# SSD output projection by seven products of quarters, and the SSD skip term written by ScalarE

## The chip, the cores and the metric

One NeuronCore of one Trainium2 chip runs the whole layer. The metric is the device time of one execution in microseconds (us), as the median of several runs. Five engines work at once, each through a list of instructions of its own, in order: TensorE (PE, matrix products into PSUM banks), VectorE (DVE), ScalarE (ACT), GpSimd (POOL) and SyncE (SP, which issues most DMAs). They wait for each other by semaphores. DMA engines move data between HBM and the on-chip memory.

## The reference

One decoder layer over 1024 tokens of width 1024, all in float32. An SSD (Mamba-2) branch and a latent attention branch are projected back to the model's width, weighed by gates, added, and projected once more (W_O); a gated feed-forward network (FFN) follows.

```python
y = ssd_chunked_scan(xs * dt[..., None], dt * a, bm, cm)
y = y + xs * d_skip[:, None]                      # the skip term
y = y.reshape(b, l, D_INNER) * jax.nn.silu(z)
y = rms_norm(y.reshape(b, l, SSD_GROUPS, D_INNER // SSD_GROUPS), ...)
...
y_ssd = ssd_mixer(...) @ w_ssd_proj[i]            # 1024 x 2048 by 2048 x 1024
y_mla = mla_mixer(...) @ w_mla_proj[i]
x = x + (g_ssd * y_ssd + g_mla * y_mla) @ w_o[i]
h = rms_norm(x, norm_ffn_g[i])
u = causal_depthwise_conv(h @ w_up[i], conv_ffn_w[i], conv_ffn_b[i])
x = x + (jax.nn.silu(u_gate) * u_val) @ w_down[i]
```

## The kernel before

Activations lie channel by channel: 128 channels on the partitions, 512 tokens (a "half") in the free dimension. A float32 product is made of three matmuls: each operand is split into a high part, rounded to the PE's fast format (a copy by ScalarE, L153), and a low part, the rest (a subtraction by VectorE or GpSimd, L154), and `mm3` (L174 to L177) adds high x high, high x low and low x high into one PSUM bank. So one k-step of a 128x512 tile is 3 matmuls, and both the weights and the activations must have been split before.

The order of the work is that in which the Python code records it, engine by engine. During the SSD scan a list `background` of generators (other projections) is advanced between the steps of the scan, so that PE has work while the scan's vector steps run; what a step of the scan takes from it is fixed by counts.

*The scan* runs over 4 groups of 512 channels (a tile `xg`, also called `chan`, of 128 x 4 x 1024) and in each over 8 chunks of 128 tokens. `ssd_inputs` prepares a chunk: eight exponents by ScalarE (L850, `seg`), a product of them with the scores on VectorE (L864), the chunk's inputs transposed and scaled (L855, L860). `ssd_output` (L885) adds into a PSUM bank `yp` on PE: 8 matmuls within the chunk (L891), and 8 for the carried state (L896). Then VectorE adds the skip term: four operations of 128x128, one for each block of channels, x = x * hds + yp (L903), and one of 128x512 that multiplies by the gate z (L905). `ssd_finish` normalizes a group's half. It writes it to HBM in `y_d`, and for half 0 of the last group it splits it in place. `first_ssd_tile` (L1052), the last piece of the background, makes the first projection tile of 48 matmuls while the last group is finished.

*The projection* (L1204 to L1231) runs over two halves, and in each over 8 tiles of output channels (`ct`). A tile takes 16 k-steps of 3 matmuls. Its weights come in two halves by `load_w`: 256 KB loads by SP into one of two buffers `wraw`, then the split. GpSimd's queue loads two tiles of gates, `gt` and `mt`; VectorE and ScalarE make the merged value from PSUM, `gt` and `mt` (L1224 to L1229) and split it (`m`, `ma`). After the tiles of a half comes *W_O* of that half (L1242 to L1277): 2 blocks of 512 columns, each 4 weight pairs (`kp`) by 4 token tiles by 2 k-steps, 192 matmuls; VectorE adds the product to the residual `big` (L1270). So the order is projection half 0, W_O half 0, projection half 1, W_O half 1. The normalization of half 0's new residual, `norm(x0)` (L1232 to L1234, scaled at L255), is recorded between the second projection and W_O of half 1, and eight transposes of its result (`quarter`) are spread over W_O of half 1 from the start. The activations of half 1 are loaded back from `y_d` by `load_act`, 16 tiles of 256 KB. The FFN behind is done by seven products of quarters already; its first weights (`w_raw`, `w_sums`) are loaded and added during these stages.

## Time and profile before

| | us |
|---|---|
| runs | 2203.98, 2197.95, 2196.79 |
| median | 2197.95 |
| profiled execution | 2203.12 |
| its span, first to last instruction | 2201.3 |

The three runs are timed executions; the page of the profile comes from one more execution, whose own time stands in the third row. All stretches and starts below count from the start of its span. In them the SSD scan lies from about 740 to 1262, the projection and W_O of both halves from 1253 to 1524, and the FFN behind. A line number Lnnn is one of the kernel before.

### The profile page before, as it was taken

What the parts mean: (1) busy time and instruction counts of PE and PEld (TensorE: products, weight loads), DVE (VectorE), ACT (ScalarE), POOL (GpSimd) and SP (SyncE); (2) the same over time, 40 slices, a digit from 0 to 9 for tenths busy, and PEclk for the clock granted to TensorE, in tenths of its full rate; (3) what the DMA queues carried; (4) which work ended last, traced back from release to release, by engine and by line L of the source; (5) the groups of instructions that cost most, each with busy time, mean ns of one, the idle gap of its engine ahead of it and who ended that gap; (6) DMA issues with size and microseconds to landing.
All of it is one profiled execution on the core that took longest, in us unless ns stands there. A gap on an engine that the chain in (4) does not pass through costs nothing. (4 is left out here: it accounts for less than half of the span.)

```text
span 2201.3 us, 30448 instructions
## 1 busy us (share of the span) xinstructions
PE 2145.3 (97%) x10844; PEld 1713.8 (78%) x10844; DVE 1446.8 (66%) x2567; ACT 1064.3 (48%) x2034; POOL 969.6 (44%) x1049
## 2 busy tenths in 40 slices
PE   8999999999999999999999999999899999999999
PEld 7877776777777887778877787887678888877787
DVE  4466756575664469898877746545876676676762
ACT  5445454555454456656564424324655455554330
POOL 2344424432443237665456311013377777744430
PEclk9999999999999999999999999999999999999999
DMA  4221111111112224645266566542132333248642
GB/s 147 69 69 46 40 53 64 50 35 55 64 48 88 93 82 148 195 151 172 92 229 212 178 224 200 166 161 95 63 119 92 111 105 110 96 138 330 258 158 82
DMA packets 121767, 268.97 MB, mean 122 GB/s; under 512 B 13520, under 2 KB 25744, under 8 KB 121616
## 3 DMA queue, kind: packets, MB, share of 16 engines
q1 hardware_dynamic: 105600, 214.47, 29.0%
q0 software_dynamic: 14528, 49.29, 6.8%
q10 hardware_dynamic: 1488, 3.28, 0.4%
q8 instruction: 85, 1.39, 0.3%
q14 instruction: 66, 0.54, 0.1%
HBM read 201.45 MB, written 65.54 MB: 121 GB/s over the span
## 5 line engine op out<-in xcount | busy, mean ns | idle before, releaser
L175 PE MATMUL lin<-h,whi 128*128 128x512 f32 x1440 | 591.6, 411 | 1.5 <-DVE lt L330 1.5
L177 PE MATMUL lin<-h,wlo 128*128 128x512 f32 x1440 | 563.7, 391 | 0.0
L176 PE MATMUL lin<-h,whi 128*128 128x512 f32 x1440 | 562.4, 391 | 0.0
L175 PEld LDWEIGHTS lin<-h,whi 128*128 128x128 f32 x1440 | 270.6, 188 | 83.9 <-issue 33.8
L177 PEld LDWEIGHTS lin<-h,wlo 128*128 128x128 f32 x1440 | 270.4, 188 | 59.8 <-POOL wlo L154 0.4
L176 PEld LDWEIGHTS lin<-h,whi 128*128 128x128 f32 x1440 | 271.5, 189 | 53.2 <-issue 6.7
L154 POOL TENSOR_TENSOR wlo<-wraw,whi 128x512 fp32r<-128x512 f32 x134 | 193.0, 1458 | 169.3 <-ACT whi L153 165.7
L153 ACT CAST whi<-wraw 128x512 fp32r<-128x512 f32 x232 | 141.1, 619 | 260.0 <-PE lin L176 111.1
L664 POOL TENSOR_TENSOR acc<-acc,e 128x512 f32<-128x512 f32 (+3 forms) x80 | 78.8, 984 | 246.1 <-ACT e L659 223.7
L659 ACT ACTIVATE e<-s 128x512 f32<-128x512 f32 (+1 forms) x192 | 93.3, 492 | 153.7 <-DVE s L657 133.1
L1140 DVE TENSOR_TENSOR xlo<-ur,xhi 128x512 fp32r<-128x512 f32 (+1 forms) x41 | 83.0, 2024 | 60.9 <-ACT xhi L1139 60.9
L154 DVE TENSOR_TENSOR wlo<-wraw,whi 128x512 fp32r<-128x512 f32 x98 | 70.0, 725 | 75.1 <-ACT whi L153 74.7
L850 ACT ACTIVATE seg<-abc,acum 128x128 f32<-128x128 f32 x256 | 80.2, 390 | 47.1 <-PE yp L891 41.0
L175 PE MATMUL dps<-tq,h 128*128 128x512 f32 x242 | 96.8, 400 | 5.8 <-DVE xr L1601 3.5
L176 PE MATMUL dps<-tq,h 128*128 128x512 f32 x242 | 96.9, 400 | 0.8 <-DVE tq L154 0.8
L177 PE MATMUL dps<-tq,h 128*128 128x512 f32 x242 | 96.4, 398 | 0.0
L812 DVE SCALAR_TENSOR_TENSOR xg<-craw,cl,xg 128x1024 f32<-128x1024 f32 x48 | 73.7, 1536 | 27.4 <-ACT xg L810 26.9
L664 DVE TENSOR_TENSOR acc<-acc,e 128x512 f32<-128x512 f32 (+3 forms) x80 | 55.1, 689 | 37.1 <-ACT e L659 36.5
L1216 POOL DMA_DIRECT2D mt<-m_d x16 | 8.6, 539 | 147.1 <-DVE gt L1225 97.1
L154 DVE TENSOR_TENSOR h<-ar,h 128x1024 fp32r<-128x1024 f32 (+1 forms) x35 | 56.4, 1616 | 25.4 <-ACT h L153 25.3
L670 PE MATMUL pv<-e,vt 128*64 128x512 f32 (+3 forms) x384 | 72.9, 498 | 0.0
L629 DVE CUSTOM_DVE_ANT_0 s<-s,negw 128x128 f32<-128x128 f32 (+3 forms) x128 | 62.3, 495 | 13.5 <-PE s L627 13.4
(617 smaller groups left out, 5225.7 us busy)
## 6 DMA issues: line engine op xcount, KB each, us to landing
wraw<-in_w_main SPq DMA_DIRECT2D x112, 256.0 KB
ur<-in_w_up SPq DMA_DIRECT2D x44, 512.0 KB
ar<-f_d SPq DMA_DIRECT2D x34, 512.0 KB
abc<-ac_d POOLq DMA_DIRECT2D x32, 512.0 KB, 5.3
wraw<-in_w_ssd SPq DMA_DIRECT2D x64, 256.0 KB
f_d<-wraw POOLq DMA_DIRECT2D x33, 256.0 KB, 2.4
g_d<-lt SPq DMA_DIRECT2D x32, 256.0 KB
z_d<-lt SPq DMA_DIRECT2D x32, 256.0 KB
```

The costliest lines, as they stand in the source:

```text
L153: S.copy(hi, raw)
L154: (eng or V).tensor_sub(lo, raw, hi.bitcast(F32))
L175: PE.matmul(ps, lhsT=ah, rhs=bh, start=first, stop=False, **more)
L176: PE.matmul(ps, lhsT=ah, rhs=bl, start=False, stop=False, **more)
L177: PE.matmul(ps, lhsT=al, rhs=bh, start=False, stop=last, **more)
L629: V.tensor_tensor_reduce(ps[:, 0:w], ps[:, 0:w], negw[:, 512 - w:512], 1.0, 2 * NEG, ALU.add, ALU.max, nm[:, j, i:i + 1])
L659: S.activation(e[:, c0:512], ps[:, 0:w], AF.Exp)
L664: (V if hd else G).tensor_tensor(accs[hd][:, c0:512], accs[hd][:, c0:512], e[:, c0:512], op=ALU.add)
L670: PE.matmul(pv[hd * 64:(hd + 1) * 64, c0:512], lhsT=vt[:, j, hd * 64:(hd + 1) * 64], rhs=es[hd][:, c0:512], start=first, stop=last)
L812: V.scalar_tensor_tensor(c, raw[:, k:k + T], col(cw + k), c, op0=ALU.mult, op1=ALU.add)
L850: S.activation(seg[:, hd, :], abc[:, hd, :], AF.Relu, bias=acum[:, c, 8 * g + hd:8 * g + hd + 1], scale=-1.0)
L1140: eng.tensor_sub(lo, r, hi.bitcast(F32))
```

## The change

*The projection.* Instead of two halves of 8 output tiles by 16 k-steps, the product is cut into quarters: the activations into channels of two kinds and tokens of two halves, the weights into two kinds of input channels and two halves of output tiles. Seven products of quarters (Winograd's form of Strassen's method) replace eight. For each, sums of quarters stand in for the activations ("forms": s22, and t1 to t4) and for the weights (differences and sums). They run in the order 1, 2, 7, 6, 5, 3, 4, each as 4 units of 8 k-steps, 24 matmuls of the same shape. The code loads raw quarters of weights three units ahead (`fetch`), prepares a unit's weights and gates one unit ahead (`prepare`), and combines the results after each (`finish_unit`).

```diff
+
+    def quarter_k(kk, h):
+        return 8 * (kk // 4) + 4 * (kk // 2 % 2) + 2 * h + kk % 2
+
+    def quarter_w(ct, h, kp):
+        return w_ssd[ct, kp].rearrange("p (g h j) c -> h p g (j c)", h=2, j=2)[h]
+
+    def load_q(ct, h):
+        hi = wpool.tile([P, KD, P], F32R, name="whi")
+        lo = wpool.tile([P, KD, P], F32R, name="wlo")
+        for kp in range(2):
+            raw = wpool.tile([P, 512], F32, name="wraw", bufs=2)
+            nc.sync.dma_start(out=raw.rearrange("p (g c) -> p g c", c=256), in_=quarter_w(ct, h, kp))
+            f = "p a b -> p (a b)"
+            split(raw, hi[:, 4 * kp:4 * kp + 4, :].rearrange(f), lo[:, 4 * kp:4 * kp + 4, :].rearrange(f), w_eng[0])
+        return hi, lo
+
+    def quarter_step(ps, w, t, kk, first):
+        mm3(ps, (w[0][:, kk, :], w[1][:, kk, :]), (t[:, 0, :], t[:, 1, :]), first and kk == 0, kk == KD - 1,
+            skip_group_check=True)
...
+            def ring():
+                turns[0] += 1
+                if turns[0] % 3 == 0:
+                    return up.tile([P, KD, P], F32, name="us", bufs=1)
+                return up.tile([P, T + 2], F32, name="ug", bufs=2)[:, 0:T].rearrange("p (k c) -> p k c", c=P)
...
+            e1, e2 = [ep.tile([P, 4, D], F32, name="x2").rearrange("p i (k c) -> p i k c", c=P) for _ in range(2)]
+            ur = [up.tile([P, KD, P], F32, name=f"ur{n}", bufs=2) for n in (1, 1, 2, 2)]
...
+            units = [(p, i) for p in (1, 2, 7, 6, 5, 3, 4) for i in range(4)]
...
+            source = {6: "t2", 5: "t1", 3: "22", 7: "t3", 4: "t4"}
+            following = {2: 7, 7: 6, 6: 5, 5: 3, 3: 4}
...
+                if p == 7:
+                    raw_q(ur[i], i, 0)
+                    rs[p, i] = ring()
+                    raw_q(rs[p, i], i + 4, 0)
+                elif p == 6:
+                    raw_q(e1[:, i], i + 4, 1)
...
+                if p in (1, 2, 4):
+                    ws[p, i] = load_q(i + 4 if p == 4 else i, 0 if p == 1 else 1)
+                    return
+                v = {6: e1[:, i], 5: ur[i], 3: rs.get((p, i)), 7: e2[:, i]}[p]
+                if p == 7:
+                    V.tensor_tensor(v, ur[i], rs[p, i], op=ALU.subtract)
+                elif p == 6:
+                    V.tensor_tensor(v, v, e2[:, i], op=ALU.subtract)
+                elif p == 5:
+                    V.tensor_tensor(v, v, e1[:, i], op=ALU.add)
+                else:
+                    V.tensor_tensor(v, v, e1[:, i], op=ALU.subtract)
+                hl = [wpool.tile([P, KD, P], F32R, name=w) for w in ("whi", "wlo")]
+                split(v.rearrange(flat), hl[0].rearrange(flat), hl[1].rearrange(flat))
...
+            for n in range(2, len(units)):
+                p, i = units[n]
+                prepare(n + 1)
+                fetch(n + 3)
+                f = following.get(p)
+                if f:
+                    t = forms.setdefault(f, [])
+                    for _ in range(min(3, KD - len(t))):
+                        t.append(load_act(t_d[source[f]], len(t) * P, slice(0, 512)))
...
+                for kk in range(KD):
+                    quarter_step(b, ws[p, i], forms[p][kk], kk, p in (1, 2, 7))
+                finish_unit(p, i)
```

`X` and `Z` are PSUM banks, four each; `finish_unit` copies X to on-chip memory after products 1, 6 and 5, adds partial products on VectorE after 2, 5 and 4, and makes a merged value with the gates after 7, 5, 3 and 4 (two steps on VectorE each). `first_ssd_tile` becomes `first_products`: the first two units, also 48 matmuls. The forms are made at the end of each group in `ssd_finish` (half 1 no longer goes to `y_d`, but for GpSimd's queue to five buffers in HBM):

```diff
-                else:
-                    nc.sync.dma_start(out=y_d[r0:r0 + P, s], in_=x[:, j, s])
+                elif half == 0:
+                    nc.sync.dma_start(out=y_d[r0:r0 + P, :], in_=x[:, j, s])
             if half:
+                s11, s21 = x[:, 0:2, 0:512], x[:, 2:4, 0:512]
+                s12, s22 = x[:, 0:2, 512:1024], x[:, 2:4, 512:1024]
+
+                def form(name, v, a=None, b=None, op=None):
+                    if op is not None:
+                        V.tensor_tensor(v, a, b, op=op)
+                    nc.gpsimd.dma_start(out=t_d[name][2 * g * P:2 * (g + 1) * P, :].rearrange("(j p) t -> p j t", p=P),
+                                        in_=v)
+
+                form("22", s22)
+                form("t3", s12, s22, s12, ALU.subtract)
+                form("t2", s11, s12, s11, ALU.add)
+                form("t4", s21, s21, s11, ALU.subtract)
+                form("t1", s22, s22, s11, ALU.subtract)
```

*The order behind it.* Both halves' W_O now follow each other after the last product. `norm(x0)` is recorded between them, as one group of four tiles (before, a tile at a time); the transposes of its result start six places later in W_O of half 1; the weight pairs of that half are taken in the order 2, 3, 0, 1; the weights of the FFN's second pair are added at its third weight pair.

```diff
+                    drain([norm(x0, x0, ep, x2ss[0], group=4)])
...
+                    for n_, kp in enumerate((2, 3, 0, 1) if half else range(4)):
...
+                            slot += i % 2
+                            if half and i % 2 and slot > 5 and nq < KD:
                                 quarter("11" if nq < 4 else "21", nq % 4, h2_raw(nq, 0), act_tile(), G)
```

*The skip term.* ScalarE writes x * hds into the PSUM bank while the chunk is prepared, and PE adds onto it; VectorE reads the bank in the multiplication by z.

```diff
+            yp = psy.tile([P, 512], F32, name="yp", bufs=2)
+            for j in range(4):
+                S.activation(yp[:, j * P:(j + 1) * P], xs[:, j, cs], AF.Copy, scale=hds[:, 4 * g + j:4 * g + j + 1])
+            return abc, seg, xdt, xde, bt, yp
...
-                              rhs=seg[:, hd, :], start=True, stop=c == 0)
+                              rhs=seg[:, hd, :], start=False, stop=c == 0, skip_group_check=True)
...
-            for j in range(4):
-                V.scalar_tensor_tensor(x[:, j, cs], x[:, j, cs], hds[:, 4 * g + j:4 * g + j + 1],
-                                       yp[:, j * P:(j + 1) * P], op0=ALU.mult, op1=ALU.add)
-            V.scalar_tensor_tensor(x[:, :, cs], zts.pop(0), 0.5, x[:, :, cs], op0=ALU.mult, op1=ALU.mult)
+            V.scalar_tensor_tensor(x[:, :, cs], zts.pop(0), 0.5, yp.rearrange("p (j t) -> p j t", t=P),
+                                   op0=ALU.mult, op1=ALU.mult)
...
+        seeded = [psy.tile([P, 512], F32, name="yp", bufs=2) for _ in range(2)]
+        for i in (0, 1, 0):
+            PE.matmul(seeded[i], lhsT=h[0][0][:, 0, 0:P], rhs=h[0][0][:, 0, :], start=True, stop=True)
```

Where the instructions stand: three places. In the kernel after, lines lie lower in the file: L153 and L154 are L154 and L155, L850 is L871, L852 is L873, L866 is L887. The first place is ScalarE around one chunk of the scan's second group (`seg` and `abc` belong to the chunk, `craw` and `lt` to the projections beside it). Before:

```order
L852 ACTIVATE seg<-seg 128x1024
L153 CAST whi<-wraw 128x512
L850 ACTIVATE seg<-abc,acum 128x128 x5
L816 ACTIVATE craw<-xg 128x1024
L850 ACTIVATE seg<-abc,acum 128x128
L329 ACTIVATE lt<-lin 128x512
L914 ACTIVATE sq__9247<-xg 128x512
L850 ACTIVATE seg<-abc,acum 128x128 x2
L852 ACTIVATE seg<-seg 128x1024
L866 ACTIVATE abc<-abc 128x1024
L153 CAST whi<-wraw 128x512
```

After, in the same group (L891 are the seeds):

```order
L871 ACTIVATE seg<-abc,acum 128x128 x3
L891 ACTIVATE yp<-xg,hds 128x128
L871 ACTIVATE seg<-abc,acum 128x128 x4
L891 ACTIVATE yp<-xg,hds 128x128
L873 ACTIVATE seg<-seg 128x1024
L887 ACTIVATE abc<-abc 128x1024
L891 ACTIVATE yp<-xg,hds 128x128
L350 ACTIVATE lt<-lin 128x512
L891 ACTIVATE yp<-xg,hds 128x128
L154 CAST whi<-wraw 128x512
L891 ACTIVATE yp<-xg,hds 128x128
L154 CAST whi<-wraw 128x512
```

The four `yp` rows of a chunk are new. They stand one by one between the chunk's exponents and the other work.

The second place is VectorE in the projection. Before, in a tile of half 0 (`gt`, `mt` are the gates, `lin` the PSUM bank, `m` the merged value, `wlo` the low part of the next weights):

```order
L1229 SCALAR_TENSOR_TENSOR m<-gt,m 128x512
L154 TENSOR_TENSOR wlo<-wraw,whi 128x512 x2
L1224 SCALAR_TENSOR_TENSOR gt<-gt,lin 128x512
L154 TENSOR_TENSOR wlo<-wraw,whi 128x512
L1225 TENSOR_TENSOR gt<-gt,mt 128x512
L154 TENSOR_TENSOR wlo<-wraw,whi 128x512
L1229 SCALAR_TENSOR_TENSOR m<-gt,m 128x512
```

After, in the units of product 7 (`x_12837` holds the differences of product 7, `x_12836` those of product 6, `h<-lt` is the low part of a form):

```order
L1318 SCALAR_TENSOR_TENSOR gt<-gt,mu 128x512
L1307 TENSOR_TENSOR x_12836<-x_12836,x_12837 128x1024
L155 TENSOR_TENSOR h<-lt,h 128x512 x2
L1251 SCALAR_TENSOR_TENSOR ma<-mu,ma 128x512
L155 TENSOR_TENSOR wlo<-x_12837,whi 128x1024
L1319 TENSOR_TENSOR mu<-gt,mt 128x512
L1307 TENSOR_TENSOR x_12836<-x_12836,x_12837 128x1024
L1251 SCALAR_TENSOR_TENSOR ma<-mu,ma 128x512
L1307 TENSOR_TENSOR x_12836<-x_12836,x_12837 128x1024
L1309 TENSOR_TENSOR ur_12838<-ur_12838,x_12836 128x1024
L155 TENSOR_TENSOR wlo<-x_12836,whi 128x1024
```

Sums of weights of 128x1024 now stand in the same queue as the splits that PE waits for.

The third place is VectorE at `norm(x0)`. Before, with the second projection's steps behind the scaling (L255):

```order
L247 SCALAR_TENSOR_TENSOR nst<-nst 128x1
L248 TENSOR_TENSOR nst<-nst 128x1
L249 SCALAR_TENSOR_TENSOR nst<-nst 128x1
L255 TENSOR_SCALAR x_13360<-x_13360,nst 128x1024 x2
L234 TENSOR_REDUCE nst<-sq_13362 128x1 x2
L154 TENSOR_TENSOR wlo<-wraw,whi 128x512
L1224 SCALAR_TENSOR_TENSOR gt<-gt,lin 128x512
L154 TENSOR_TENSOR wlo<-wraw,whi 128x512
L1225 TENSOR_TENSOR gt<-gt,mt 128x512
```

After, between the two W_O (L276 is the scaling, `wlo` the low part of W_O's weights, L1223 a copy of a transposed tile, L1424 the residual's sum):

```order
L268 SCALAR_TENSOR_TENSOR nst<-nst 128x4
L269 TENSOR_TENSOR nst<-nst 128x4
L270 SCALAR_TENSOR_TENSOR nst<-nst 128x4
L276 TENSOR_SCALAR x_14048<-x_14048,nst 128x1024 x4
L155 TENSOR_TENSOR wlo<-wraw,whi 128x512 x4
L1223 TENSOR_SCALAR x_14048<-dps,cl 128x4x128
L155 TENSOR_TENSOR wlo<-wraw,whi 128x512
L1424 TENSOR_TENSOR x_14049<-dps,x_14049 128x512
```

Behind the scaling of all four tiles now stand the low parts of W_O's own weights.

More of the change, by code (lines that the diff above doesn't have):

```diff
@@ L88, in tile_hybrid_layer @@
     l_d = dram.tile([4 * MH, 256], F32, name="l_d")
-    y_d = dram.tile([2 * D, T], F32, name="y_d")
+    y_d = dram.tile([2 * D, 512], F32, name="y_d")
+    t_d = {n: dram.tile([D, 512], F32, name=f"t_d{n}") for n in ("22", "t1", "t2", "t3", "t4")}
     z_d = dram.tile([2 * D, T], F32, name="z_d")
@@ L884, in ssd_output @@
         def ssd_output(g, c, inp, st):
-            abc, seg, xdt, _, _ = inp
+            abc, seg, xdt, _, _, yp = inp
             cs = slice(c * P, (c + 1) * P)
-            yp = psy.tile([P, 512], F32, name="yp", bufs=2)
             for j in range(4):
@@ L1016, in y_step @@
                         lt.tile([P, 512], F32, name="lt")
-                    staged.append(raw_load(y_d, k, hs_(0), raw))
+                    staged.append(raw_load(y_d, k, slice(0, 512), raw))
             def one(w, ct, half, side=None):
@@ L1201, in hp_tiles, with gates @@
                 return [act_tile().rearrange("p a (b c) -> p (a b) c", c=P) for _ in range(2)]
-            m0 = [em.tile([P, 2, 512], F32R, name="ma", bufs=3) for _ in range(3)]
+            def gates(ct, half):
+                gt = em.tile([P, 512], F32, name="gt")
+                nc.gpsimd.dma_start(out=gt, in_=g_d[ct * P:(ct + 1) * P, hs_(half)])
+                mt = em.tile([P, 512], F32, name="mt")
+                nc.gpsimd.dma_start(out=mt, in_=m_d[ct * P:(ct + 1) * P, hs_(half)])
+                return gt, mt
@@ new lines, in tile_hybrid_layer, with fetch @@
+            Z = [None] * 4
+            units = [(p, i) for p in (1, 2, 7, 6, 5, 3, 4) for i in range(4)]
+            ws, rs, gm, forms = {}, {}, {}, {}
+            forms[1], forms[2] = [[ya0[quarter_k(kk, h)] for kk in range(KD)] for h in range(2)]
+            source = {6: "t2", 5: "t1", 3: "22", 7: "t3", 4: "t4"}
+            following = {2: 7, 7: 6, 6: 5, 5: 3, 3: 4}
+            place = {7: (0, 0), 5: (4, 1), 3: (0, 1), 4: (4, 0)}
+            def fetch(n):
+                if n >= len(units):
+                    return
[6 more added lines that the diff above has]
+                    raw_q(e1[:, i], i + 4, 1)
+                elif p == 3:
+                    rs[p, i] = ring()
+                    raw_q(rs[p, i], i, 1)
@@ new lines, in tile_hybrid_layer @@
+            for i in range(2):
+                finish_unit(1, i)
+            for n in range(2, 5):
+                fetch(n)
+            prepare(2)
+            for n in range(2, len(units)):
+                p, i = units[n]
+                prepare(n + 1)
[5 more added lines that the diff above has]
+                        t.append(load_act(t_d[source[f]], len(t) * P, slice(0, 512)))
+                if p in (1, 6, 5, 3):
+                    b = X[i]
+                else:
+                    if p != 4:
+                        Z[i] = bank6()
+                    b = Z[i]
+                for kk in range(KD):
+                    quarter_step(b, ws[p, i], forms[p][kk], kk, p in (1, 2, 7))
+                finish_unit(p, i)
@@ L1205, in tile_hybrid_layer @@
+            bigs = [ep.tile([P, 4, D], F32, name="x2") for _ in range(2)]
             for half in range(2):
+                nc.sync.dma_start(out=bigs[half], in_=x[hs_(half), :].rearrange("(i p) c -> p i c", p=P))
+            ms = ma + ml
+            for half in range(2):
+                s = hs_(half)
                 if half:
-                    w_raw(q0, loaded)
-                    w_raw(q1, loaded)
-                s = hs_(half)
-                ya = ya0 if half == 0 else [load_act(y_d, k * P, s) for k in range(16)]
@@ L1231, in tile_hybrid_layer @@
-                if half:
+                    m12 = [em.tile([P, 2, 512], F32R, name="mu", bufs=4) for _ in range(4)]
+                    for i in range(4):
+                        merged(mr[i], m12[i][:, 0, :], m12[i][:, 1, :])
+                    ms = m12 + m22
                     x0 = [x2b[0][:, i, :] for i in range(4)]
-                    drain([norm(x0, x0, ep, x2ss[0])])
-                big = ep.tile([P, 4, D], F32, name="x2")
+                    drain([norm(x0, x0, ep, x2ss[0], group=4)])
@@ L1251, in tile_hybrid_layer @@
                             split(raw, wh[:, k, :], wl[:, k, :], w_eng[0])
-                        if half and (ch, kp) in ((1, 0), (1, 1)):
-                            q = pairs[kp]
+                        if not half and ch and n_ > 1:
+                            if n_ == 2:
+                                m22 = []
+                                w_raw(q0)
+                                w_raw(q1)
+                            for i in range(2 * n_ - 4, 2 * n_ - 2):
+                                m22.append(em.tile([P, 2, 512], F32R, name="ma", bufs=4))
+                                merged(us[i][:, 0, :], m22[i][:, 0, :], m22[i][:, 1, :])
+                        if half and ch and n_ in (0, 2):
+                            q = pairs[n_ // 2]
                             q.a = w_split(q.r1, hp_tiles(), V)
-                            w_sums(q, act_tile().rearrange("p a (b c) -> p (a b) c", c=P).bitcast(F32) if kp else None)
-                        if half and (ch, kp) == (1, 3):
+                            w_sums(q, act_tile().rearrange("p a (b c) -> p (a b) c", c=P).bitcast(F32) if n_ else None)
+                        if half and (ch, n_) == (1, 3):
                             q2.a = hp_tiles()
```

106 lines of the change are left out of this document (65 added, 41 removed).

## Prediction

> **What bounds the kernel now.** The page of the profile comes first: its span, the busy shares, the granted clock and the shares of the chain of waits.
>
> ```profile
> span 2201.3 us, 30448 instructions
> PE 2145.3 (97%) x10844; PEld 1713.8 (78%) x10844; DVE 1446.8 (66%) x2567; ACT 1064.3 (48%) x2034; POOL 969.6 (44%) x1049
> PEclk9999999999999999999999999999999999999999
> PE 23%; DVE 2%; DMA 1%; issue 0%; POOL 0%; ACT 0%; SPq 0%; DVEq 0%; ACTq 0%
> ```
>
> TensorE (PE) is busy for 97% of the span at nearly the full clock, and the chain that the page could follow back is mostly PE. A share over the whole span says little about one stage, so the second view is busy time by stage. After the stretch come its length and, with instruction counts in brackets, PE, weight loads, VectorE (DVE), ScalarE (ACT) and GpSimd (POOL), then clock, DMA share and GB/s.
>
> ```profile
> 740.00:1110.00 370.00, 367.04 (x2144) 294.82 (x2143) 307.20 (x434) 213.33 (x391) 200.34 (x172) 1.00 0.42 134
> 1110.00:1240.00 130.00, 126.25 (x778) 101.20 (x777) 94.66 (x170) 67.50 (x139) 69.04 (x77) 1.00 0.66 213
> 1265.90:1342.40 76.50, 76.50 (x339) 63.33 (x338) 36.83 (x53) 23.38 (x39) 14.54 (x23) 1.00 0.66 216
> 1342.40:1389.30 46.90, 45.23 (x193) 35.65 (x192) 25.67 (x48) 22.10 (x42) 1.08 (x2) 1.00 0.55 178
> 1389.30:1476.40 87.10, 87.10 (x386) 72.12 (x386) 42.36 (x101) 24.72 (x44) 6.46 (x12) 1.00 0.55 181
> 1476.40:1524.10 47.70, 47.63 (x226) 39.10 (x225) 28.42 (x36) 20.32 (x37) 19.49 (x13) 1.00 0.32 100
> ```
>
> The first two rows are the SSD scan. The next four are the projection of half 0 (without its first tile, which ran before 1265.9), W_O of half 0, the projection of half 1 and W_O of half 1. Both projection rows have PE busy for their whole length, and VectorE for under half of it. So the projection is matmul time and nothing else. A projection half has 8 tiles of 48 matmuls, 384, and 87.10 / 384 is 0.2268 us each. The timeline of PE shows that pitch directly: each starts 0.22 to 0.23 us after the one ahead, although one lasts 0.39.
>
> ```profile
> 1341.72 0.39 PE L175 MATMUL lin<-h,whi 128*128 128x512 f32 x1
> 1341.95 0.39 PE L176 MATMUL lin<-h,whi 128*128 128x512 f32 x1
> 1342.17 0.39 PE L177 MATMUL lin<-h,wlo 128*128 128x512 f32 x1
> ```
>
> **The change, part by part.** *Matmuls.* Before: 2 halves x 8 tiles x 16 k-steps x 3 = 768. After: 7 products x 4 tiles x 8 k-steps x 3 = 672. The 96 that go are worth 96 x 0.2268 = **-21.8 us**. Two of the 28 new units (24 matmuls each) run where the first tile of 48 ran; the other 26 take 624 x 0.2268 = 141.5 us, and a unit takes 5.44. The three matmuls that seed the two output banks cost **+0.7** with their turn of the pipeline (3 x 0.23).
>
> *VectorE in the stage.* These rows price the added sums; the window of the third is 1265.9 to 1342.4:
>
> ```profile
> L1140 DVE TENSOR_TENSOR wlo<-us,whi 128x1024 fp32r<-128x1024 f32 x2 | 2.5, 1225 | 1.1 <-ACT whi L1139 1.1
> L1140 DVE TENSOR_TENSOR xlo<-ur,xhi 128x1024 fp32r<-128x1024 f32 x20 | 49.9, 2496 | 51.3 <-ACT xhi L1139 51.3
> L154 DVE TENSOR_TENSOR wlo<-wraw,whi 128x512 fp32r<-128x512 f32 x28 | 20.3, 729 | 27.2 <-ACT whi L153 27.1
> 1389.72 0.69 DVE L1270 TENSOR_TENSOR x<-dps,x 128x512 f32<-128x512 f32 x1
> 1390.32 0.69 DVE L154 TENSOR_TENSOR wlo<-wraw,whi 128x512 fp32r<-128x512 f32 x1
> ```
>
> A 128x512 operation lasts 0.69 to 0.73 and the next starts 0.60 later. By the order after, the stage has about 112 of these: 40 low parts of the forms' splits, 20 of weights, 32 gate steps, 12 adds of partial products and 8 low parts of the merged values. It has 32 of 128x1024, 16 differences of weights and 16 low parts, at 1.23. That is 112 x 0.60 + 32 x 1.23 = 107 us of 141.5. VectorE has cover of a third, as a mean. It stands in one queue, though: a difference that waits for its raw quarters holds the low part of the weights behind it, and PE waits for that. By hand through the first units of the third product, the low part comes 0.5 to 1 us after PE is ready. I count 1 us there.
>
> *Loads in the stage.* From the fifth to the ninth of the 28 units SP asks for three units of weights at 512 KB, four pairs of raw quarters at 1 MB and 11 tiles of forms at 256 KB; POOL asks for four tiles of gates at 256 KB. That is 1.57 + 4.19 + 2.88 + 1.05 = 9.7 MB in 5 x 5.44 = 27.2 us, or 357 GB/s. Three rows show what the DMA engines gave:
>
> ```profile
> 1310.00:1325.00 15.00, 15.00 (x68) 12.43 (x67) 7.82 (x11) 4.17 (x8) 4.91 (x5) 1.00 0.97 365
> 1341.00:1362.00 21.00, 19.76 (x82) 14.71 (x81) 11.46 (x18) 9.50 (x16) 1.08 (x2) 1.00 0.75 240
> 2050.00:2090.00 40.00, 40.00 (x174) 32.44 (x173) 27.52 (x22) 15.63 (x21) 21.49 (x13) 1.00 0.88 326
> ```
>
> At 365 GB/s everything is in time; at 240 / 0.75 = 320, the second row's rate if its engines had been full, it takes 30.3 us, 3.1 late. The quarters are read in runs of 1 KB, as W_O's weights are (second row), but loads issued ahead of this stretch take off some: 2 us. If nothing went faster than the mean 240 GB/s of that row, 9.7 MB would take 40.4 us, **+13**. With the 1 us above: **+3** for stalls, between 0 and +14.
>
> The Trainium skill, in "DMA: Bandwidth & Descriptors", section "Measured (HBM→SBUF, 128 partitions, SWDGE, issued from GpSimd)", asks for transfers of 1 MiB or more for 75% of the peak, and gives 138 GB/s at 64 KB and 341 at 1 MB. For these 256 KB pieces an estimate halfway, 240 GB/s, gives the +13 too. By that rule the change would keep half of its gain. The 365 GB/s above, with pieces of 256 KB to 2 MB in flight together, speaks against it.
>
> *W_O.* The row of W_O in half 0 has 46.90 us for 192 matmuls, 43.5 at the pitch: 3.4 us of stalls while SP loads 16 tiles of y_d (4 MB) ahead for half 1. These loads go, and VectorE's splits with them. I take **-2**, between 0 and -3.4. Now both W_O halves stand back to back, and norm(x0) falls between them. Its scaling overwrites x in place, so it waits for the store of x:
>
> ```profile
> 1390.43 0.38 SPq L1280 DMA_DIRECT2D x_d<-x  x1
> 1397.94 1.42 DVE L255 TENSOR_SCALAR x<-x,nst 128x1024 f32<-128x1024 f32 x2 [4.37 <-DMA x_d<-x]
> ```
>
> W_O of half 0 ended at E = 1389.3, where the window's row ends; the scaling began at E + 8.6, and VectorE waited 4.37 us for the store. Before, a projection tile of 48 matmuls (10.9 us) with its weights ready covered it. After, four scalings (0.67 each apart, half the 1.42 of two) end at E + 11.3, and VectorE's low part of the third weight pair of W_O stands behind them. A pair lasts 24 matmuls, 5.44 us, so PE needs it at E + 10.9. It is ready at about E + 12: **+1.2**, between 0 and the 8 of a wait without cover.
>
> *The scan.* VectorE loses the four skip operations of each chunk, ScalarE gains four, and 16 sums of forms and 20 stores are new.
>
> ```profile
> L903 DVE SCALAR_TENSOR_TENSOR xg<-xg,hds,yp 128x128 f32<-128x128 f32 x128 | 36.8, 339 | 10.9 <-PE yp L896 8.7 <-PE yp L891 2.1
> L850 ACT ACTIVATE seg<-abc,acum 128x128 f32<-128x128 f32 x240 | 75.2, 390 | 41.0 <-PE yp L891 41.0
> L867 DVE TENSOR_TENSOR abc<-abc,chan 128x1024 f32<-128x1024 f32 x28 | 36.2, 1291 | 11.5 <-ACT abc L866 11.5
> abc<-ac_d POOLq DMA_DIRECT2D x32, 512.0 KB, 5.3
> ```
>
> VectorE: -36.8 + 16 x 1.29 = -16 us. ScalarE: 128 x 0.39 = +50 us beside 281 busy of 500, so 66% after. The row of L850 has it idle for 41 us because of PE: ScalarE has room. PE is busy 493 of the 500 us, so relief of VectorE can bring at most 7, and a sum of forms at a group's end (four at 1.29, and a store of 5.3 us to be waited for before the last) can hold VectorE about 5 us, three times where PE still has scan work. Nothing shows which of the two wins; bounds -3 and +10, taken **+1.5**.
>
> **Sum:** -21.8 + 0.7 + 3 - 2 + 1.2 + 1.5 = -17.4 us. The profiled execution took 2203.1 us (span 2201.3), 5.2 above the median 2197.95; the difference carries over, so the time is 2197.95 - 17.4 = **2180.5, say 2181**. At the good ends of all terms (-21.8 + 0.7 + 0 - 3.4 + 0 - 3 = -27.5) it is 2170.
>
> **Rivals.** (a) *Loads bound the stage*: +14 in place of +3, 2191. For it: two raw buffers for the weights and 357 GB/s asked. Against: every raw quarter is issued three units (16 us) ahead. (b) *The boundary of W_O*: +8 in place of 1.2, 2188; for it the wait of 4.37 us, against it the two weight pairs that are ready ahead. (c) *VectorE becomes the bound, and the kernel is slower.* The second L1140 row shows the same 128x1024 operation at 2.50 us. The slowest 128x512 steps of the projection of half 0 were these:
>
> ```profile
> L1225 DVE TENSOR_TENSOR gt<-gt,mt 128x512 f32<-128x512 f32 x7 | 5.9, 842 | 0.0
> ```
>
> At 0.84 and 2.50 the stage has 112 x 0.84 + 32 x 2.50 = 174 us, 32.6 over PE, in place of the +3: -17.4 - 3 + 32.6 = +12, 2210. It decides against the gain once VectorE's work passes 141.5 + 17.4 = 159 us. For it: the price is in the trace. Against: POOL computes three operations in the whole stage after, while it runs tensor work where the 2.50 stands. The Trainium skill, "VectorE: DVE Perf Modes", section "Two Vector instructions with no wait between them", has the second SBUF operand read through an interface shared with GpSimd; the 1225 and 2496 ns agree with that. (d) *ScalarE's seeds hold the scan*: PE's first matmul of a chunk's output now waits for four of them. If none is hidden, 32 chunks x 4 x 0.39 = +50 in place of the scan's 1.5, and the kernel is slower too, 2229; if a quarter is not hidden, +12.5, 2191.5. The 41 us in which ScalarE waited for PE speak against the first.
>
> **How the numbers follow.** About 0.3%, 6.6 us, is what a measurement of this kernel can tell from no change. Forecast (2170 to 2188) 0.57; (a) 0.17; (b) 0.10; (c) 0.06; (d) 0.10, half of it slower than 2204. Faster by over 0.3% is below 2191.4: all of the forecast and of (b), half of (a): 0.76. Slower, above 2204.5: (c) and half of (d): 0.11. The rest, half of (a) and of (d), 0.13, lies within. The range goes from 2171 to 2200: up to (a) and (b) with some of what lies behind them, without the slower cases and the last of the good ends.
>
> **What would show it.** Right: 672 matmuls of 128x512 from the first to the last product at 0.227 apart, PE gaps of 1 us or so at the third product only, and the adds of partial products hidden. (a) shows as PE waiting for low parts whose raw loads land over 10 us after issue, (b) as a gap 11 us into W_O of half 1, (c) as VectorE over 90% in the stage with 1024-wide operations above 2 us, (d) as PE waiting for ScalarE's seeds (L891 after). The forecast is wrong if PE's pitch in the stage differs from 0.227, or the scan grows by more than 10 us.

## The result and the profile after

The changed kernel took 2207.22 us (median of 7 runs, 2205.47 to 2210.33), the kernel before 2201.49 us (7 runs, 2196.79 to 2205.65). The ratio is 1.0033, with a 95% interval from 1.0019 to 1.0046: slower by a third of a percent, where 17 us faster was forecast. The profiled execution took 2206.37 us. One run of e6 and one of e8 below, at 2882 and 2975 us with a granted clock of 0.68 and 0.66, are left out of the medians and ratios.

The page of the changed kernel, its span and busy shares:

```profile
span 2204.6 us, 30301 instructions
PE 2132.6 (97%) x10751; PEld 1697.8 (77%) x10751; DVE 1463.1 (66%) x2447; ACT 1110.5 (50%) x2174; POOL 970.7 (44%) x1069
```

PE has 93 instructions fewer, as the change says, but is busy only 12.7 us less, not 21.8, and idle 16 us more (span less busy time: 72.0 against 56.0). Busy time by stage, with the columns of the prediction's table: the 26 units of the projection, then W_O of both halves.

```profile
1281.40:1437.00 155.60, 146.31 (x625) 117.30 (x625) 111.31 (x143) 61.16 (x95) 24.65 (x41) 0.99 0.79 263
1437.00:1528.90 91.90, 91.17 (x418) 75.17 (x418) 55.05 (x87) 38.95 (x76) 19.07 (x13) 1.00 0.37 121
```

Four differences make up the 3.3 us of the span. The units start at 1281.4 where the same point of the kernel before lay at 1265.9: **+15.5** up to the end of the scan. The stage takes 155.6 us where the two projection rows had 76.5 + 87.1 = 163.6: **-8.0**. W_O takes 91.9 against 46.9 + 47.7: **-2.7**. The FFN behind takes 675.7 against 677.2: **-1.5**.

PE's waits in the scan, before and after (what waited, for whom, us in total, times, longest):

```profile
PE sn L874 <- DVE bt L863: 4.4, 3, 2.3
```

```profile
PE sn L898 <- DVE bt L884: 11.3, 5, 4.6
PE lin L176 <- DVE rb L1068: 3.4, 1, 3.4
PE xp L861 <- DVE xg L838: 1.4, 2, 0.7
```

In both, the matmul of a chunk's state (`sn`) waits for VectorE's copy `bt`, the last of a row of VectorE steps. After, it waits 6.9 us more, and two waits are new. The whole scan, from its first state matmul to its last transposes, before and after:

```profile
795.08:1260.27 465.19, 456.74 (x2780) 365.41 (x2778) 387.24 (x617) 267.84 (x515) 261.16 (x242) 1.00 0.52 167
```

```profile
795.26:1275.50 480.24, 462.62 (x2780) 368.34 (x2779) 369.82 (x501) 301.69 (x634) 256.84 (x257) 0.99 0.53 171
```

Of the 15.0 us between them PE is idle for 9.2 more (17.6 against 8.5). For the other 5.9 it counts as busy, with the same 2780 instructions. That is mostly the clock. Around the longest gap of the projection, 3.8 us at 1302:

```profile
1300.00:1302.20 2.20, 0.02 (x1) 0.02 (x1) 0.04 (x1) 0.69 (x2) 0.00 (x0) 0.97 0.87 301
1302.20:1305.40 3.20, 3.20 (x8) 2.48 (x9) 1.34 (x2) 1.03 (x2) 0.00 (x0) 0.50 0.39 118
1305.40:1308.60 3.20, 3.20 (x15) 2.63 (x14) 1.75 (x3) 0.66 (x2) 0.00 (x0) 0.99 0.76 251
```

For 3.2 us behind the gap the granted clock is 0.50, and PE does 8 matmuls where it does 15 right after. It counts as busy in both rows. This gap of 3.8 us so costs about 5.4 (3.8 and seven matmuls at 0.227). In the scan the granted clock stands at 0.50 for some 3.4 us each at the gaps at 1022, 1151 and 1200, and nowhere in the scan before: by half of that time, an estimate, 5.1 of the 5.9 us.

### The profile page after: what moved, and what is told of

The parts are those of the page before. It is cut to its first block, busy times and chain, and to the rows that moved or that the text cites. A ratio compares the mean times of both kernels' runs of the same rounds, so it can differ in the third digit from the quotient of the medians.

```text
span 2204.6 us, 30301 instructions
## 1 busy us (share of the span) xinstructions
PE 2132.6 (97%) x10751; PEld 1697.8 (77%) x10751; DVE 1463.1 (66%) x2447; ACT 1110.5 (50%) x2174; POOL 970.7 (44%) x1069
## 5 line engine op out<-in xcount | busy, mean ns | idle before, releaser
L176 PE MATMUL lin<-h,whi 128*128 128x512 f32 x1248 | 519.1, 416 | 4.3 <-DVE rb L1068 3.4
L178 PE MATMUL lin<-h,wlo 128*128 128x512 f32 x1248 | 490.6, 393 | 0.4 <-POOL wlo L155 0.4
L177 PE MATMUL lin<-h,whi 128*128 128x512 f32 x1248 | 489.5, 392 | 0.0
L176 PEld LDWEIGHTS lin<-h,whi 128*128 128x128 f32 x1248 | 235.8, 189 | 80.5 <-issue 33.5
L155 POOL TENSOR_TENSOR wlo<-wraw,whi 128x512 fp32r<-128x512 f32 x134 | 189.9, 1434 | 202.9 <-ACT whi L154 200.5
L178 PEld LDWEIGHTS lin<-h,wlo 128*128 128x128 f32 x1248 | 235.3, 189 | 53.5 <-POOL wlo L155 0.8
L177 PEld LDWEIGHTS lin<-h,whi 128*128 128x128 f32 x1248 | 236.4, 189 | 46.1 <-issue 7.0
L154 ACT CAST whi<-wraw 128x512 fp32r<-128x512 f32 x192 | 116.2, 618 | 171.8 <-PE lin L177 69.4
L871 ACT ACTIVATE seg<-abc,acum 128x128 f32<-128x128 f32 x256 | 81.5, 389 | 42.2 <-PE yp L914 35.3
L176 PE MATMUL dps<-h,whi 128*128 128x512 f32 x244 | 96.4, 395 | 6.2 <-ACT whi L154 4.5
L178 PE MATMUL dps<-h,wlo 128*128 128x512 f32 x244 | 96.4, 395 | 4.8 <-DVE wlo L155 4.7
L177 PE MATMUL dps<-h,whi 128*128 128x512 f32 x244 | 95.5, 392 | 0.0
```

Source lines behind the costliest of these rows:

```text
L154: S.copy(hi, raw)
L155: (eng or V).tensor_sub(lo, raw, hi.bitcast(F32))
L176: PE.matmul(ps, lhsT=ah, rhs=bh, start=first, stop=False, **more)
L177: PE.matmul(ps, lhsT=ah, rhs=bl, start=False, stop=False, **more)
L178: PE.matmul(ps, lhsT=al, rhs=bh, start=False, stop=last, **more)
L871: S.activation(seg[:, hd, :], abc[:, hd, :], AF.Relu, bias=acum[:, c, 8 * g + hd:8 * g + hd + 1], scale=-1.0)
```

## Where the time went: four places in the trace

**1. ScalarE at a group's change.** VectorE (first) and ScalarE (second) of the changed kernel, when the scan goes from the first group to the second:

```profile
904.50 1.23 DVE L888 TENSOR_TENSOR abc<-abc,chan 128x1024 f32<-128x1024 f32 x1 [3.23 <-ACT abc L887]
...
907.03 0.28 DVE L884 COPY bt<-sp 128x128 f32<-128x128 f32 x1
```

```profile
900.70 0.37 ACT L891 ACTIVATE yp<-xg,hds 128x128 f32<-128x128 f32 x1 [0.53 <-DVE xg L838]
901.01 1.26 ACT L871 ACTIVATE seg<-abc,acum 128x128 f32<-128x128 f32 x4
902.18 0.35 ACT L891 ACTIVATE yp<-xg,hds 128x128 f32<-128x128 f32 x1
902.47 1.04 ACT L873 ACTIVATE seg<-seg 128x1024 f32<-128x1024 f32 x1
903.42 1.04 ACT L887 ACTIVATE abc<-abc 128x1024 f32<-128x1024 f32 x1
```

A seed (L891) waits for the last tile of the new group's convolution, and the exponents that VectorE needs stand behind it and between other seeds. ScalarE works almost without a pause here. VectorE stands 3.23 us for `abc`, and the copy `bt` comes after that. Before, it stood 0.55 us at the same place:

```profile
900.31 1.23 DVE L867 TENSOR_TENSOR abc<-abc,chan 128x1024 f32<-128x1024 f32 x1 [0.55 <-ACT abc L866]
```

**2. VectorE at a group's end.** The last sum of a group (L993, t1) overwrites s22 and must wait until its store has landed:

```profile
1191.18 1.22 DVE L993 TENSOR_TENSOR xg<-xg 128x1024 f32<-128x1024 f32 x1 [5.22 <-DMA t_d<-xg]
...
1195.06 4.31 DVE L885 TENSOR_TENSOR seg<-seg,sm__11924 128x1024 f32<-128x1024 f32 x1
1199.29 0.67 DVE L1068 SCALAR_TENSOR_TENSOR rb<-rb,lin 128x512 f32<-128x512 f32 x1
```

**3. GpSimd's queue** in the same stretch:

```profile
1192.71 0.71 POOL L994 DMA_DIRECT2D t_dt<-xg  x1 [5.74 <-DVE xg L993]
1193.43 0.76 POOL L936 TENSOR_TENSOR sq__11897<-sq__11897 128x256 f32<-128x256 f32 x1
...
1195.32 2.49 POOL L155 TENSOR_TENSOR wlo<-wraw,whi 128x512 fp32r<-128x512 f32 x2
1197.75 0.57 POOL L1063 DMA_DIRECT2D chan<-g_d  x1
1198.35 1.91 POOL L903 TENSOR_TENSOR st<-st,cdec 128x512 f32<-128x512 f32 x1
```

GpSimd stands 5.74 us at the store of t1, for the sum that VectorE makes late. Its tensor work then runs in a bunch, and beside it VectorE's product `seg`, 1.2 us at its shortest, lasts 4.31. VectorE's `rb` comes behind, and PE waited for that 3.4 us (row above).

**4. Loads in the stage.** ScalarE, SP and GpSimd ahead of the gap at 1302:

```profile
1301.51 0.62 ACT L154 CAST whi<-wraw 128x512 fp32r<-128x512 f32 x1 [5.63 <-DMA wraw<-in_w_ssd]
```

```profile
1293.10 0.54 SPq L191 DMA_DIRECT2D wraw<-in_w_ssd  x1
```

```profile
1292.23 0.57 POOL L1244 DMA_DIRECT2D gt<-g_d  x1 [6.44 <-DMA wraw<-in_w_ssd]
1292.79 0.55 POOL L1246 DMA_DIRECT2D mt<-m_d  x1
1293.34 0.54 POOL L1244 DMA_DIRECT2D gt<-g_d  x1
1293.86 0.54 POOL L1246 DMA_DIRECT2D mt<-m_d  x1
```

The second unit of product 2 needs weights that SP asked for at 1293.10; ScalarE got them at 1301.51, 8.4 us later. GpSimd's queue had waited 6.44 us, by its row for a load of weights to land. It came free at 1292.23, just ahead of SP's request, and asked for four tiles of gates, 1 MB, which product 7 needs 20 us later.

This load is one of two causes of PE's waits in the stage. The other, as large in all, is VectorE's low parts of the weights:

```profile
PE dps L178 <- DVE wlo L155: 4.7, 5, 2.4
PE dps L176 <- ACT whi L154: 4.5, 2, 3.8
```

## The experiments

The first table has all runs in order. The scan is counted from its first state matmul to its last transposes, the stage from there to the first matmul of the FFN that has sums as weights (`lin<-tq,us`), some 35 us behind W_O. Both are from the timeline of PE in the profiled execution, us.

| run | median | ratio to before (95%) | scan | stage and W_O |
|---|---|---|---|---|
| before | 2199 to 2202 | | 465.2 | 299.1 |
| changed | 2207.22 | 1.0033 (1.0019 to 1.0046) | 480.2 | 289.0 |
| e1 skip alone | 2210.03 | 1.0048 (1.0030 to 1.0066) | 477.9 | 299.2 |
| e2 seven products alone | 2205.78 | 1.0030 (1.0016 to 1.0043) | 477.3 | 287.7 |
| e3 last sum later | 2216.60 | 1.0080 (1.0059 to 1.0102) | 488.1 | 289.4 |
| e4 more raw buffers | 2214.29 | 1.0069 (1.0054 to 1.0084) | 484.0 | 293.8 |
| e5 e2, store of s22 by SP | 2201.91 | 1.0015 (1.0000 to 1.0030) | 479.6 | 293.8 |
| e6 e2 without sums | 2200.69 | 1.0005 (0.9990 to 1.0021) | 476.4 | 288.2 |
| e7 e2, gates by SP | 2196.82 | 0.9989 (0.9979 to 0.9998) | 477.2 | 280.7 |
| e8 e5 and e7 | 2197.89 | 0.9986 (0.9974 to 0.9998) | 479.6 | 281.1 |
| e9 e7, all stores by SP | 2194.66 | 0.9974 (0.9964 to 0.9984) | 473.5 | 280.1 |
| e10 e7, all stores by ScalarE | 2196.18 | 0.9981 (0.9970 to 0.9991) | 476.2 | 284.2 |
| e11 e1, first seeds by VectorE | 2205.34 | 1.0025 (1.0014 to 1.0037) | 470.7 | 298.2 |
| e12 changed, gates and stores by SP | 2200.43 | 1.0000 (0.9988 to 1.0012) | 479.7 | 280.2 |
| e13 e9 without sums | 2185.66 | 0.9930 (0.9915 to 0.9945) | 467.2 | 280.1 |
| e14 e9, sums spread | 2211.72 | 1.0044 (1.0027 to 1.0061) | 492.2 | 281.7 |
| e15 e9, sums by GpSimd | 2204.93 | 1.0025 (1.0014 to 1.0036) | 477.0 | 287.2 |

The last two columns are one execution each. That of e5 took 2210.0 us, 8.1 above the median of its runs; e1's lay 6.4 and e10's 3.5 above theirs, e2's 5.8, e7's 4.1, e9's 3.8 and e12's 3.4 below. So a few us of these columns can belong to the execution. Runs that differ only in the gates, which are loaded behind the scan, agree in the scan within 0.1 us (e2 and e7, e5 and e8).

### Each half of the change alone: e1, e2

The edit of e1 is the skip term's part of the diff on the kernel before; that of e2 is its removal from the changed kernel.

> The kernel before with the skip term alone moved to ScalarE (seeds, three seed matmuls, one multiplication by VectorE). Theory A (ScalarE's longer queue at the group changes delays abc, then VectorE's copy bt, then PE): about 8 to 11 us slower than before, with PE waiting 5 us more in all at the sn matmul behind VectorE's copy than before's 4.4. Theory B (the stall of the scan comes from the forms and their stores): within 2 us of before, waits at sn near 4.4 us.

> The changed kernel with the skip term back on VectorE as before. Theory A: 8 to 11 us faster than the changed kernel, so about 2196 to 2199 where that has 2207, 2 to 5 us faster than before. Theory B: within 3 us of the changed kernel.

Theory A was right for e1 (+10 us, and gaps of 3.0, 2.4 and 5.6 us at `sn`) and wrong for e2, which was only 1.4 us faster than the changed kernel. The three gaps of e1 stand in the changed kernel too (3.0, 2.4 and 4.6 us). Each half alone makes the scan 12 to 13 us longer, both together 15: their losses do not add up. Both put work at the end of one group and the start of the next, so that one can cover the other. So both theories were half right, and the seven products have a cost in the scan of their own.

### Two edits that failed: e3, e4

```diff
+                yield                                  # e3
                 form("t1", s22, s22, s11, ALU.subtract)
...
+            raw = raws[kp] if raws else wpool.tile([P, 512], F32, name="wraw", bufs=2)   # e4; raws: two mr tiles
```

> The changed kernel with the last form of a group (t1, which overwrites s22) one scan step later than the others, so that VectorE need not stand until the store of s22 has landed. If that stand (5.2 us in group 3) is what held PE for 3.4 us at 1200 and then halved its clock for 3.5 us: 4 to 6 us faster than the changed kernel, and no PE gap above 1 us there. If the wait is hidden and another instruction was late: within 1 us.

> The changed kernel with every other unit of weights of products 1 and 2 loaded into two further raw buffers (the idle mr tiles), four to six in all in place of two. Theory L (latency: a unit's load cannot start until the unit ahead is split): the PE gap of 3.8 us at 1302 with its 1.9 us of slow clock goes, 5 to 6 us faster. Theory R (rate: the DMA engines give no more in this stretch): the gap moves to a later unit and the time is within 2 us of the changed kernel.

Both made it slower. In e3 the sum waited no longer, but the convolution of the next group but one starts only after the last sum; it began later and PE stood 5.1 us for its result at the next group's change (`xp`, 229 us after the first state matmul). In e4 ScalarE and the loads, which SP issues, waited for the forms' stores (the second row in us in total, times, longest):

```profile
1290.57 1.07 ACT L1325 COPY mu<-lin 128x512 f32<-128x512 f32 x2 [15.84 <-DMA t_dt<-xg]
```

```profile
SPq L191 <- DMA t_dt<-xg: 14.0, 1, 14.0
```

The tiles borrowed as raw buffers lie where the scan's `xg` lay, and were free only when the forms' stores had landed; the loads began 11 us later and PE stood 11.1 us. Neither run answers its question.

### What the forms cost: e5, e6, and the gates: e7, e8

```diff
+                    q = nc.sync if name == "22" else nc.gpsimd        # e5
+                    q.dma_start(out=t_d[name][...], in_=v)
...
-                    if op is not None:                                # e6
-                        V.tensor_tensor(v, a, b, op=op)
...
-                nc.gpsimd.dma_start(out=gt, in_=g_d[ct * P:(ct + 1) * P, hs_(half)])   # e7, the same for mt
+                nc.sync.dma_start(out=gt, in_=g_d[ct * P:(ct + 1) * P, hs_(half)])
```

> The seven products with the skip term on VectorE (e2), and the store of s22 issued by SP instead of GpSimd. Theory W (e2's gap of 7.3 us in group 3 comes from t1 overwriting s22: GpSimd, busy with tensor work, issued the store 5 us late, and VectorE stood 5.8 us for it): the gap falls under 2 us, the scan gets 6 to 9 us shorter than e2's, the time about 2198. Theory V (the four sums of a group take VectorE too long by themselves): the scan stays within 2 us of e2's.

> e2 without VectorE's four sums per group: the quarters are stored as they are, so the output is wrong; the stores and everything behind them stay. Nothing is overwritten any more, so VectorE has neither the sums (16 x 1.3 us) nor the wait. Theory W: the scan as in e5 or 1 to 3 us shorter. Theory V: the scan 9 to 12 us shorter than e2's, e5's not. If the stores alone load the scan (GpSimd's queue, the DMA engines), even this one stays over 3 us longer in the scan than before.

> e2 with the gates loaded by SP in the order of its queue instead of GpSimd, which runs ahead and asks for four tiles (1 MB) just when the weights of product 2 are loaded. Theory C (those loads share the engines with the weights that are needed at once): the gap at the second unit of product 2 (1.6 us in e2, 3.8 in the changed kernel) goes, and the stage from the last transposes of the scan to the FFN gets 3 to 5 us shorter than e2's 287.7. Theory R (what is asked of the DMA engines in the stage is too much whatever the order): within 1.5 us.

> e5 and e7 together: if both mechanisms are right and do not cover each other, the sum of both gains, about 2194; it would be the first version below the kernel before.

e5 disproved theory W as the whole cause: the gap of 7.3 us fell to 3.3, but another in the first group grew from 1.2 to 5.0, and the scan was no shorter (479.6 against 477.3). e6, even without sums, kept 11 us of the scan's loss. It shows the third place again, without any wait of t1. VectorE and GpSimd at the end of the first group:

```profile
937.41 1.22 DVE L888 TENSOR_TENSOR abc<-abc,chan 128x1024 f32<-128x1024 f32 x1
938.54 6.98 DVE L833 SCALAR_TENSOR_TENSOR chan<-craw,cl,chan 128x1024 f32<-128x1024 f32 x1
945.45 0.28 DVE L868 SCALAR_TENSOR_TENSOR sm__9582<-sp,cn 128x128 f32<-128x128 f32 x1
```

```profile
938.58 0.74 POOL L936 TENSOR_TENSOR sq__9529<-sq__9529 128x256 f32<-128x256 f32 x1
939.27 1.28 POOL L155 TENSOR_TENSOR wlo<-wraw,whi 128x512 fp32r<-128x512 f32 x1
...
943.40 1.03 POOL L900 TENSOR_TENSOR st<-st,cdec 128x512 f32<-128x512 f32 x1
```

The operation that lasts 6.98 us here lasts 1.27 two rows on. It starts with the first of GpSimd's six tensor operations, which follow each other without a pause behind the stores, and ends 1.1 us after the last of them. The Trainium skill, "VectorE: DVE Perf Modes", section "Two Vector instructions with no wait between them", has the second SBUF operand of VectorE read through an interface shared with GpSimd; these rows agree.

That the stores alone gathered GpSimd's work is not shown. The kernel before has five tensor operations of GpSimd without a pause at the same place, and VectorE's operation is lengthened there too, by less; two of GpSimd's take 2.27 and 2.02 us there:

```profile
936.53 3.12 DVE L812 SCALAR_TENSOR_TENSOR chan<-craw,cl,chan 128x1024 f32<-128x1024 f32 x1
```

e7 bears theory C out. The load of weights at the same place now reaches ScalarE 3.1 us after SP asked for it, not 8.4 as in the changed kernel or 6.3 as in e2:

```profile
1287.29 0.55 SPq L191 DMA_DIRECT2D wraw<-in_w_ssd  x1
```

```profile
1290.40 0.62 ACT L154 CAST whi<-wraw 128x512 fp32r<-128x512 f32 x1 [0.33 <-DMA wraw<-in_w_ssd]
```

Its stage, from the third unit to W_O:

```profile
1275.40:1424.10 148.70, 144.50 (x625) 116.36 (x624) 111.44 (x143) 61.77 (x95) 7.46 (x9) 1.00 0.83 275
```

It is 148.7 us long, against 155.6 in the changed kernel, and no PE gap above 0.9 us is left in it. Nearly all that PE still waits there (4.2 us) ends with a low part by VectorE:

```profile
PE dps L178 <- DVE wlo L155: 3.7, 6, 0.9
```

The stage with W_O is 7.0 us shorter than e2's, more than the 3 to 5 expected. This is the first version that is faster than the kernel before, if by 0.1% only. The gates also left GpSimd's way of issuing; a later request by GpSimd was not tried, so the share of each is open. e8 added nothing to e7, where about 2194 was expected.

### Stores, seeds, sums: e9 to e15

```diff
-                    nc.gpsimd.dma_start(out=t_d[name][...], in_=v)
+                    nc.sync.dma_start(out=t_d[name][...], in_=v)      # e9; e10: nc.scalar
...
+                if c < 2:                                             # e11, in place of ScalarE's seed
+                    V.tensor_scalar(yp[:, j * P:(j + 1) * P], xs[:, j, cs], hd, None, op0=ALU.mult)
```

> e7 (seven products, skip on VectorE, gates by SP) with all five stores of the forms issued by SP. Theory P (in e2 and e6 GpSimd stands in its queue for VectorE's forms, its tensor work then runs bunched, and VectorE's two-operand operations last 4 to 7 us beside it): the long operations go, the scan gets 5 to 9 us shorter than e7's 477, the time about 2190. If the traffic of the stores is what costs: the scan stays within 3 us of 477.

> The same with ScalarE issuing the five stores. Theory P: GpSimd is relieved as in e9, but ScalarE's queue now waits for VectorE's forms, and its exponents stand behind: shorter than e7 in the scan by 0 to 6 us, not as good as e9.

> The skip term alone (e1), with the seeds of the first two chunks of each group written by VectorE. Theory A' (ScalarE is the late one only at a group's change, where the seeds wait for the new group's convolution and hold its exponents): the three losses at the sn matmul (3.0, 2.4 and 5.6 us) shrink below 1.5 each, the scan is 6 to 10 us shorter than e1's 477.9, the time about 2202. If the seeds cost everywhere: the scan stays above 473.

> The changed kernel itself (skip on ScalarE) with the gates and all five stores issued by SP, so e9 with the seeds back on ScalarE. If the three causes add up (gates in the stage, stores in the scan, seeds on ScalarE at a group's change): 4 to 9 us slower than e9's 2194.7 and 5 to 9 us faster than the changed kernel's 2207, so 2198 to 2202, with the gap of about 3 us at the sn matmul of the first group's change (112 us after the first) that e9 does not have. If the seeds cost nothing beside the stores: within 2 us of e9.

e9 took 3.7 us off e7's scan, where 5 to 9 were expected, and no operation of VectorE in it lasts above 2.32 us any more (3.59 in e7, 3.12 before). So the long operations go, as theory P says; that the 3.7 us come from them is not shown, and by the medians e9 and e7 can't be told apart. e9 has the lowest median of the kernels that compute the reference, 0.9974 of the kernel before. e10's scan is 1.0 us shorter than e7's, within what was expected; its time can't be told from e9's. e11 took 7.2 us off e1's scan, within the 6 to 10 expected, so the seeds cost at a group's change above all. The time, 2205.3, stayed above the 2202 expected, and the gaps did not all fall below 1.5 us: they are 2.6, 1.6 and 3.4 now, two of them at another instruction (PE's transposes `xp`, which wait for VectorE's convolution, behind which the seeds now stand). e12 is 5.8 us slower than e9 by the seeds alone, with the gap of 3.0 us at the first group's change back. It is 6.8 us faster than the changed kernel, but the table has all of that in the stage (280.2 against 289.0), where the gates are; its scan is as long as the changed kernel's (479.7 against 480.2). Both numbers lie within what was expected of a sum of three causes, and yet the causes do not add up: with the seeds on ScalarE, the stores on SP's queue brought nothing in the scan.

e13 is e9 with the `V.tensor_tensor` of the forms left out, e14 has a `yield` ahead of each sum after the first and advances the work at a group's end in two more steps of the scan, e15 has `G.tensor_tensor` for the sums.

> e9 without VectorE's four sums per group (the quarters are stored as they are; the output is wrong). If the sums and the wait of t1 are the rest: the scan falls from e9's 473.5 us to within 3 of before's 465.2. If the traffic of the stores is the rest: it stays above 470.

> e9 with each of a group's four sums a step of the scan apart. If VectorE's burst of four sums ahead of the next chunk's copy bt is what holds PE (gap of 3.8 us at 152, 3.5 at 350): gaps below 2 us there, the scan 2 to 5 us shorter than e9's 473.5, about 2191. If the convolution of the next group but one, which waits for the last sum, is the late one instead: a gap at a group's change as in e3 and a scan as long as e9's or longer.

> e9 with the four sums of a group computed by GpSimd in place of VectorE. If the place in VectorE's queue is what costs: the gaps at 152 and 350 us after the first state matmul go, the scan falls from 473.5 to 466 to 469 us, the time to 2186 to 2190. If GpSimd's sums hold VectorE's two-operand operations (rows of 4 to 7 us beside GpSimd's work in the changed kernel and in e6) or its own queue gets late: operations of VectorE above 3 us, and a scan as long as e9's or longer.

e13 shows what the sums hold. PE's longest waits in the scan, of e9 and then of e13:

```profile
PE sn L895 <- DVE bt L884: 7.3, 2, 3.8
PE lin L176 <- DVE chan L1068: 2.3, 1, 2.3
```

```profile
PE sn L895 <- DVE bt L884: 2.9, 3, 1.5
PE lin L176 <- DVE lt L351: 2.0, 1, 2.0
```

Without the sums the scan falls to 467.2 us, 2 above before, with PE idle in it for as long as before (8.5 us), and the kernel to 2185.66 us, 15 below before, of the 21.8 that the matmuls promised. This is not the changed kernel: it leaves out the sums that the result needs, and its skip term is VectorE's. It can't tell the sums' own time from the wait for a landing, which goes with them. The stores' traffic, still all there, costs at most the 2 us. e14 and e15 made it slower: spread sums delay the next convolution (PE stood 6.5 us for it), and the gap at 152 us grew from 3.8 to 7.9. On GpSimd a sum lasts 2.75 us in the mean, and VectorE's operations last up to 3.5.

## Why the prediction was wrong, step by step

- **Matmuls, -21.8:** right. 624 matmuls stand in the 26 units, and the pitch between gaps is 0.227 us. In e13 the stage with W_O is 19.0 us shorter than before.
- **Loads in the stage, +3, taken between 0 and +14:** a term that was mis-sized. The stage has 155.6 us for 141.5 of matmuls, +14.1. That this is the end of the range, and the size of the first rival, is chance: loads are only a part of it. PE is idle for 9.3 us, 4.5 of it behind late loads, which I had at 2, and 4.7 for VectorE's low parts, which I had at 1. The slow clock behind the longest gap adds 1.6, and in the rest PE counts as busy. The rival's reason, the rate of the loads, does not fit the longest gap either. Between 1290 and 1305 us the engines gave 177 to 247 GB/s in stretches of 5 us, but at shares of 0.55 to 0.77, so they were not full. I had argued that every raw quarter is issued three units ahead. The load that came late was not one of these: it was a load of `wraw`, asked for about 5 us before PE needed it, with 1 MB that nobody needed yet beside it. With the gates in SP's order the stage lost 7.2 us (148.7 less 141.5). From 1310 to 1350 us the engines were nearly full, at shares of 0.94 to 1.07 and 303 to 362 GB/s; whether the rate holds VectorE's low parts back there stays open. An estimate by the Trainium skill's rule of large transfers ("DMA: Bandwidth & Descriptors", section "Measured (HBM→SBUF, 128 partitions, SWDGE, issued from GpSimd)") gave nearly the right size, +13, by chance: the pieces were as small in e7, which lost about half of that.
- **W_O, -2 + 1.2:** -2.7 measured. The wait behind `norm(x0)` came where it was forecast, at the low part behind the scaling, and cost 0.7 us of PE. Whether the order of the weight pairs covered the rest was not tried alone.
- **The scan, +1.5 with bounds -3 and +10:** the step that failed; +15.0, past the 10 that the prediction itself had named as a sign of being wrong. It weighed each engine's sum of work over the scan: VectorE gains 16 us, ScalarE has 41 idle. VectorE's gain came true (387.24 to 369.82 us busy in the rows of the scan), and PE lost nonetheless. At a group's change and end VectorE, ScalarE and GpSimd stand in one chain to PE, and the change put work of each exactly there: seeds ahead of exponents, stores that GpSimd waits with, sums with a wait for a landing. I had named a hold of 5 us at a group's end, three times, and set it against VectorE's gain; even my upper bound is less than three such holds. What each kind of work costs depends on what else stands there. The seeds make the scan 12.7 us longer alone (e1), 6.2 on top of e9 (e12) and 2.9 on top of e2 (the changed kernel). The stores on SP's queue take off 3.7 us without the seeds (e9 against e7) and 0.5 with them (e12). Leaving out the sums takes off 6.3 us with the stores on SP (e13) and 0.9 with them on GpSimd (e6). So the kinds are shown, and a share of the 15 us for each is not.
- **Rival (d), the seeds:** right in kind. It was priced by four seeds that a matmul waits for; what waited was the exponents behind the seeds, and no wait of PE in the scan ends with a seed.
- **Rival (c), VectorE the bound of the stage:** fell. VectorE was busy 111.3 of 155.6 us there. But PE waited for VectorE's low parts as long as for the loads.
- **The clock was missing from the sum.** Each gap was priced at its own length; the slow clock behind the longer ones adds about 5 us in the scan and 1.6 in the stage.

## What to carry to other kernels

Work that is moved off a busy engine is not priced by the receiver's idle time over a stage, but by what stands behind it in the receiver's queue at the moment when the chain to the bound engine runs through there. A queue that only issues loads, as GpSimd's did in the projection, runs ahead as soon as its buffers are free; if these loads are not needed soon, they should stand in a queue whose order keeps them behind the urgent ones, which brought 7 us here (e7). A store that has to wait holds up the work behind it in its queue. Moving the stores to SP's queue took 3.7 us off the scan of the seven products alone and nothing off the changed kernel's, so such a move has to be tried with the rest of the change in place.

## What the runs showed of the hardware

Two things were not expected. First, gaps of PE are followed by a slow clock. Of 35 gaps of 3.3 us or more between 740 and 1620 us, in the two kernels and fifteen runs, 33 were followed within 10 us by at least four matmuls 0.36 to 0.5 us apart, against 33 of 67 gaps from 2 to 3.2 us and 28 of 92 from 1 to 1.9. (A short gap can lie close to a longer one, so the last number is too high if anything.) The clock row above has 0.50 for 3.2 us, which costs about 1.6 us beyond the gap. Some slow stretches are longer: in e2, at its gap of 7.3 us, the clock is 0.50 for 10 us:

```profile
1179.20:1189.20 10.00, 4.92 (x17) 3.62 (x19) 7.49 (x9) 1.66 (x3) 5.54 (x7) 0.50 0.75 290
```

Second, a two-operand operation of VectorE can last as long as GpSimd's unbroken tensor work beside it: 6.98 us in e6 where 1.27 is usual. GpSimd's operations kept their own time in that stretch. In the kernel before, both sides were slowed at the same place: 3.12 us on VectorE, 2.27 and 2.02 on GpSimd. What decides between the two was not tried.
